# Fixed background steps late in the gate and up product, a sine chain cut in three, and pinned first splits of the down product

## The chip, the cores and the metric

The kernel runs on one core of one Trainium2 chip. The metric is the device time of one execution in microseconds, the median of several runs. "PE" is TensorE's matmul stream, "DVE" VectorE, "ACT" ScalarE, "POOL" GpSimd and "SP" SyncE. POOL and SP are used here almost only to issue transfers.

## The reference, cut to what matters

One encoder layer on 256 tokens with 2048 features, in float32: a mixer of four groups (gated linear attention, a Fourier mixer, a long convolution and a short one), cross attention to 256 memory tokens, and a gated feed-forward of width 5632.

```python
def hyena_filters(feats, w1, b1, w2, b2, w3, freq, decay):
    h = jnp.sin(freq * (feats @ w1 + b1))
    h = jnp.sin(freq * (h @ w2 + b2))
    h = h @ w3
    ...                                   # window, and the transform of both orders

def swiglu(h, w_gate_up, w_down):
    gate, up = jnp.split(h @ w_gate_up, 2, axis=-1)
    return (jax.nn.silu(gate) * up) @ w_down

    x = x + mix @ w_out[l]
    x = x + cross_attention(rms_norm(x, norm_g[l, 1]), ...)
    x = x + swiglu(rms_norm(x, norm_g[l, 2]), w_gate_up[l], w_down[l])
return rms_norm(x, final_norm_g)
```

The two places that the change touches are the two sines of the filters (early in the kernel) and the hand-over inside `swiglu`, where the product of gate and up becomes the left operand of down.

## The kernel before, in words

**Splitting.** Every float32 product is made of three float32r matmuls: each operand is cut into a high part `h` (rounded by an ACT cast) and a low part `l` (what is left, a DVE subtraction), and PE adds `h*h`, `h*l` and `l*h`. The weights arrive as 1 MB slabs (16 blocks of 128x128) in `raw` tiles through SP's queue. A slab is two items of 1024 columns, and `Stream.split` (L140 to L149) makes an item's `wh` with ACT (L146) and its `wl` with DVE (L147). Some slabs (`seven`) are also added up with each other on DVE (L176), for products that save one matmul group in eight. `Stream.look` makes items as far ahead as there are buffers: three in pool `wp`, two more in `wp2` for the slabs of gate and up and the first two of down.

**Order.** The program is written once in Python, and a list scheduler then fixes each engine's order. Each engine works in that order and waits where an operand is not there. An instruction may be moved ahead of others that were written earlier, unless `keep_place(mark)` (L323) was called: it ties each instruction written since the mark to the one written before it on the same engine. The items of `seven` slabs are tied in this way; those of the other slabs are not.

**Background work.** Work that is not on the way of the current product is a Python generator in `Background` (L231). After each matmul group the code calls `poll`, which steps a generator whose time has come, but only while `owed`, the DVE time that was promised and not yet covered by PE time, is under 0.9. `drain` steps generators to their end, whatever is owed. `dve(n, ops)` adds n/960 + 0.155 per operation to `owed`, and `pe(us)` takes PE time off.

**Gate and up** (`gate_up`, L932). Eleven steps `j` of 512 columns each. In a step, `i` runs over eight slabs of the contraction; from `j` = 1 on, three of the eight (`i` = 1, 3, 5) are `seven` slabs. A step ends with `combine` and `finish` on DVE and ACT, which leave 512 features of silu(gate) * up, turned, in the DRAM tensor `hidden` (L507, eight POOL transfers). Three generators run beside it:
- `turned` (`turn`, L1041): sixteen DVE transposes of the residual (L1048), each followed by four POOL stores to `xrows` (L1051), and then four pairs of POOL loads back into `res` (L1055). One step of the generator is one transpose, or one pair of loads.
- `early` (`fetch`, L909): it loads `hidden` back in tiles of 128 features (L917, into one of 11 `tmp` tiles) and splits each into down's left operand `f[k]` (ACT cast L310, DVE subtraction L302). It loads three tiles ahead of the one that it splits; one step of the generator is one split, and the splits are tied by `keep_place`. It makes `f[0]` to `f[15]`; the slots are `act` and `f` tiles.
- `end` (`finish` of the step before).

**Down** (class `Down`, L1063). The plan takes `k` = 0 to 31 in plain groups of four, then six `unit`s for `k` = 32 to 43. `start` (L1178) runs the first two plain groups (`k` = 0 to 7) while the pools of gate and up are still there, and drains `end`, `turned` and `early`. `begin` (L1187) fetches `f[16]` to `f[43]` in the same manner, six ahead, and `ready(k + 4)` steps that generator before each `k`.

**The sines** (`Hyena.sine`, L1315). Nine DVE operations on 64 partitions (bias, frequency, range reduction, clamp: L1320 and L306) and an ACT sine, written in one piece and tied in their places. `filters` (L1360) calls it twice, after the matmuls of L1371 and L1384, and goes on with four transforms (`dft`, L1341, matmuls L1339).

```python
    def poll(self):
        for e in list(self.q):
            if self.owed < OWED and self.now >= e[1]:
                self.step(e)
```

Of the kernel before, what the change touches and what calls it, by code (L numbers as in the profile page):

```python
# [18 lines left out]
ALU = mybir.AluOpType  # L19
# [4 lines left out]
R = 256  # L24
# [16 lines left out]
LATE = 12  # L41

AHEAD = 2

EARLY = 16

# [2 lines left out]
def sevens(j):  # L49

    return (1, 3, 5) if j else (5,)
# [19 lines left out]
DOWN = GU // 16 + 16 * DFF // 1024  # L71
# [4 lines left out]
def seven(slab):  # L76

    j, i = divmod(slab - GU // 16, 8)
    return slab in UNITS if slab >= DOWN else j >= 0 and i in sevens(j)
# [11 lines left out]
V_B1, V_B2, V_FR = 129, 130, 131  # L91
# [3 lines left out]
TWO_PI_1 = 6.28125  # L95
TWO_PI_2 = float(np.float32(2 * math.pi - 6.28125))
TWO_PI_3 = float(2 * math.pi - 6.28125 - float(np.float32(2 * math.pi - 6.28125)))
MAGIC = float(np.float32(1.5 * 2 ** 23))
PI_LO = float(np.nextafter(np.float32(math.pi), np.float32(0)))


class Stream:
# [48 lines left out]
    def make(self):  # L151

        nc, (slab, part) = self.nc, self.todo
        n = 16 * slab + 8 * part
        if n >= NBLK - HELD:
            parts = [(self.places.pop(0)) for _ in range(2)]
            r = self.raw(slab)[:, part * 1024:part * 1024 + 1024]
            for a, (wh, wl) in zip((0, 512), parts):
                nc.scalar.copy(wh, r[:, a:a + 512])
                nc.vector.tensor_tensor(out=wl, in0=r[:, a:a + 512], in1=wh.bitcast(F32), op=ALU.subtract)  # L160
            self.bg.dve(1024, 2)
            self.items.append((None, parts))
            self.todo = (slab + part, 1 - part)
            return True
        pool = self.free(slab)
        if pool is None:
            return False
        raw = self.raw(slab)
        at = 48 if any(a <= n < b for a, b in ROWS) else 8
        r = raw[:, part % 2 * 1024:part % 2 * 1024 + 1024]  # L170
        if not seven(slab):
            self.split(pool, at, r, [0, 256, 512, 1024] if n == 0 else [0, 512, 1024] if n == 8 else [0, 1024])
            self.todo = (slab + part, 1 - part)
            return True
        mark = len(nc.cur_bb.bb.instructions)
        op = lambda out, a, b, what=ALU.subtract: nc.vector.tensor_tensor(out=out, in0=a, in1=b, op=what)  # L176
        self.split(pool, at, r, [0, 512] if part == 0 else [0, 1024])
        b11, b12, b22, b21 = (raw[:, a:a + 512] for a in range(0, 2048, 512))
        if part == 0:
            blk = raw.rearrange("p (b c) -> p b c", b=4)  # L180
            op(r.rearrange("p (b c) -> p b c", b=2), blk[:, 0:3:2, :], blk[:, 1:2, :].to_broadcast([P, 2, 512]))
            self.bg.dve(1024)
        elif part == 1:
            op(b22, b22, b11, ALU.add)
            op(b21, b21, b22)
            self.bg.dve(1024, 2)
        self.keep(mark)
        self.todo = (slab + part // 3, (part + 1) % 4)
        return True
# [41 lines left out]
class Background:  # L231
# [20 lines left out]
    def step(self, e):  # L252
        w = next(e[0], self)
        if w is self:
            self.q.remove(e)
        else:
            e[1] = self.now + self.owed + (w or LAG)

    def poll(self):
        for e in list(self.q):  # L260
            if self.owed < OWED and self.now >= e[1]:
                self.step(e)

    def drain(self, g=None, others=False):
        while True:
            q = [e for e in self.q if g is None or e[0] is g]
            if not q:
                break
            for e in list(self.q) if others else q:
                self.step(e)  # L270


class Block:
# [605 lines left out]
    def mlp(self):  # L879
        tc, nc, act, st = self.tc, self.nc, self.act, self.st  # L880
        slots = lambda pool, n, a, b: [pool.tile([P, 512], F32R, name=f"{n}{i}") for i in range(a, b)]
        with tc.tile_pool(name="fp", bufs=1) as fp:
# [3 lines left out]
            with tc.tile_pool(name="wp2", bufs=2) as wp2, tc.tile_pool(name="rawx", bufs=1) as st.rawx, \  # L886
                    tc.tile_pool(name="sw", bufs=1) as sw, tc.tile_pool(name="gp", bufs=1) as gp:
                self.gap(sw, 192)
                st.pools.append([wp2, 2, DOWN + AHEAD])
                d = Down(self, f)  # L890
# [41 lines left out]
    def gate_up(self, sw, gp, f):  # L932

        nc, st = self.nc, self.st
# [25 lines left out]
        def unit(i, cs, ps, start, stop, c0, c1):  # L960

            whole = lambda k, r: [self.h3[k][:, a + r * P:a + (r + 1) * P] for a in (0, R)]
            formed = lambda n: [x[:, n * P:(n + 1) * P] for x in sums[i]]
            for (p, a, own), b in zip(((ps[0], whole(2 * i, 0), True), (cs[0][1], formed(3), False),
                                       (cs[0][0], whole(2 * i + 1, 0), False), (ps[1], formed(0), True), (ps[2], formed(2), True),
                                       (ps[3], formed(1), True), (cs[1][0], whole(2 * i + 1, 1), False)),
                                      st.take_forms("w_gate_up", (2 * i, 2 * i + 1), c0, c1), strict=True):
                self.part(p, *a, *b, own and start, own and stop)
                self.bg.poll()
# [36 lines left out]
        turned = self.bg.add(self.turn())  # L1006
        early = end = None
        for j in range(DFF // 512):
            cols = [j * 512, DFF + j * 512]
            banks = [self.gbank, self.bank]  # L1010
            cs = [[banks[j % 2]() for _ in cols] for _ in range(2)]
            if j == 1:
                early = self.bg.add(self.fetch(f, 0, EARLY, 3, 2.0))
            for i in range(8):
                if j == 0 and i == 6:
                    for g in ready:
                        self.bg.drain(g)
                if i == 1 and end:
                    self.bg.drain(end)
                if i in sevens(j):  # L1020
                    if i == sevens(j)[0]:
                        if j == 0:
                            self.bg.drain(forms)
                        ps = [banks[1 - j % 2]() for _ in range(4)]
                    unit(i, cs, ps, i == sevens(j)[0], i == sevens(j)[-1], *cols)
                    if i == sevens(j)[-1]:
                        s = [[gp.tile([P, 512], F32, name=f"{n}{r}", tag=f"{n}{r}") for n in "gh"] for r in range(2)]
                        last = combine(ps, s)
                        self.bg.add(last)
                    continue  # L1030
                for k in (2 * i, 2 * i + 1):
                    for c in range(2):
                        wh, wl = st.take("w_gate_up", k, cols[c], 4)
                        for r in range(2):
                            self.part_rows(cs[r][c], r, self.h3[k], wh, wl, k == 0, k == KT - 1)
                            self.bg.poll()
            self.bg.drain(last)
            end = self.bg.add(finish(j, cs, s))
# [24 lines left out]
class Down:  # L1063
# [114 lines left out]
    def start(self, end, turned, early):  # L1178
# [3 lines left out]
        self.open(PLANS[0], b.bank)  # L1182
        self.run(0, PLANS[0][:AHEAD], None)
        for x in (end, turned, early):
            b.bg.drain(x)

    def begin(self, sd):  # L1187
# [5 lines left out]
        n, self.rest = (1 + max(i for i, x in enumerate(plan) if x[0] == "unit") for plan in PLANS)  # L1193
        self.run(0, one[AHEAD:n], b.gbank)
        todo = [b.bg.add(self.combine(0))]
# [61 lines left out]
class Hyena:  # L1257
# [57 lines left out]
    def sine(self, p, bias):  # L1315

        b, nc = self.b, self.b.nc
        a, n = b.tmp()[0:64, :], b.tmp()[0:64, :]
        v = lambda c: b.vec[0:64, c:c + 1]
        ts = lambda out, in0, s1, op0, s2=None, op1=None: nc.vector.tensor_scalar(  # L1320
            out=out, in0=in0, scalar1=s1, scalar2=s2, op0=op0, **({} if op1 is None else {"op1": op1}))
        b.bg.dve(6 * 200, 6)
        mark = b.mark()
        ts(a, p, v(bias), ALU.add)
        ts(a, a, v(V_FR), ALU.mult)
        ts(n, a, 1.0 / (2 * math.pi), ALU.mult)
        ts(n, n, MAGIC, ALU.add)
        ts(n, n, MAGIC, ALU.subtract)
        for c in (TWO_PI_1, TWO_PI_2, TWO_PI_3):
            b.stt(a, n, -c, a, ALU.mult, ALU.add)  # L1330
        ts(a, a, PI_LO, ALU.min, -PI_LO, ALU.max)
        nc.scalar.activation(a, a, AF.Sin)
        b.keep_place(mark)
        return a
# [25 lines left out]
    def filters(self):  # L1360
        b, nc, t = self.b, self.b.nc, self.b.t
# [7 lines left out]
        p = b.bank()  # L1369
        mark = b.mark()  # L1370
        nc.tensor.matmul(p[0:64, 0:R], c33[:, R:R + 64], c33[:, 0:R], start=True, stop=True)  # L1371
        b.keep_place(mark)
        h = self.sine(p[0:64, 0:R], V_B1)
        for _ in range(4):
            yield
        b.split2(self.tabh, self.tabl, fwd)
# [5 lines left out]
        p = b.bank()  # L1382
        mark = b.mark()
        nc.tensor.matmul(p[0:64, 0:R], w2, h, start=True, stop=True)  # L1384
        b.keep_place(mark)
        h = self.sine(p[0:64, 0:R], V_B2)
        hs = self.k2.tile([P, R], F32R, name="hs", tag="hs", bufs=1)
        nc.scalar.copy(hs[0:64, :], h)
        b.tt(hs[64:P, :], h, hs[0:64, :].bitcast(F32), ALU.subtract)
# [2 lines left out]
        for o in range(2):  # L1392
# [12 lines left out]
            for r in range(2):  # L1405
                hd = []
                for d in range(2):
                    wh, wl, dc = ws[d]
                    p = b.bank()
# [428 lines left out]
```

## Time and profile before

| what | value |
|---|---|
| median of 3 runs | 1467.46 us (1466.33 to 1468.1) |
| the profiled execution's own time | 1466.78 us |
| its span, first to last instruction | 1464.7 us |
| PE busy | 1442.2 us, 98% of the span |
| DVE busy | 1192.9 us, 81% |
| ACT busy | 842.9 us, 58% |
| POOL busy | 171.5 us, 12% |
| mean granted TensorE clock | 0.997 |

The view of stages gives, for a stretch of the span, the busy time of each engine with the number of instructions in brackets, the granted clock, the share of the DMA engines and GB/s. The view of groups has busy time, mean ns of one, and the idle time before them with what ended it. The timeline has start, duration, engine, line, operation, output and inputs, and in square brackets how long the engine sat idle before and who ended that. A matmul of 512 columns is shown as 0.39 us long, but the next one starts 0.23 us after it: they are pipelined, and the end is modelled. Gate and up run from about 752 to 1210 us, down from 1209.9 to the end.

### The profile page before, as it was taken

How to read it: one execution, taken by the hardware profiler on the slowest of the kernel's cores; microseconds unless marked ns; L12 is line 12 of the kernel's file. 1: busy time of each engine (PE TensorE's matmuls, PEld its weight loads, DVE VectorE, ACT ScalarE, POOL GpSimd, SP SyncE). 2: the span in 40 equal slices, each digit the busy share in tenths (PEclk: the TensorE clock that was granted, in tenths of full speed). 3: DMA queues.
4: the chain of work that ended last, by engine and by line, in shares of the span. 5: the costliest groups of instructions: out<-in, count | busy, mean ns of one | idle time of the engine just before them, and what ended most of it. 6: DMA issues, size and time to landing. Idle time of an engine off the chain costs nothing.

```text
span 1464.7 us, 19727 instructions
## 1 busy us (share of the span) xinstructions
PE 1442.2 (98%) x7219; PEld 1217.2 (83%) x7219; DVE 1192.9 (81%) x1748; ACT 842.9 (58%) x1250; POOL 171.5 (12%) x294
## 2 busy tenths in 40 slices
PE   9999999999999999999999999999999999899997
PEld 7878888898899888888888888888888887688886
DVE  6588768778868767877788999999999996798875
ACT  6556655466656656666565555555555555555554
POOL 0220100000000001100013252111110116100000
PEclk9999999999999999999999999999999999999999
DMA  9976564454636555545566787556565667465554
GB/s 349 354 255 205 202 212 166 151 185 155 209 126 209 197 199 201 191 165 183 191 209 206 246 278 248 203 203 230 200 220 211 229 213 239 170 223 181 228 201 144
DMA packets 57393, 307.16 MB, mean 210 GB/s; under 512 B 9773, under 2 KB 11470, under 8 KB 25680
## 3 DMA queue, kind: packets, MB, share of 16 engines
q1 hardware_dynamic: 45920, 281.11, 54.7%
q0 software_dynamic: 10944, 24.14, 5.5%
q8 instruction: 56, 0.92, 0.2%
q10 hardware_dynamic: 432, 0.66, 0.1%
q14 instruction: 41, 0.34, 0.1%
HBM read 291.71 MB, written 14.16 MB: 209 GB/s over the span
## 4 chain that ended last, share of the span: by engine, by line
PE 93%; DMA 2%; DVE 2%; POOL 1%; issue 1%; ACT 1%; SPq 0%; POOLq 0%; ACTq 0%; DVEq 0%
PE pg L424 18%; PE pg L476 13%; PE pg L477 13%; PE pg L475 13%; PE pg L425 10%; PE pm L477 6%; PE pm L476 6%; PE pm L475 6%; DMA tmp<-hidden 1%; PE pm L1339 1%; DVE wl L147 1%; PE pg L421 1%; PE pg L422 1%; PE pm L872 1%; PE pm L845 1%
## 5 line engine op out<-in xcount | busy, mean ns | idle before, releaser
L146 ACT CAST wh<-raw 128x1024 fp32r<-128x1024 f32 (+1 forms) x589 | 590.4, 1013 | 469.6 <-PE pg L477 154.3
L147 DVE TENSOR_TENSOR wl<-raw,wh 128x1024 fp32r<-128x1024 f32 (+1 forms) x589 | 683.5, 1175 | 178.4 <-ACT wh L146 171.6
L424 PE MATMUL pg<-act,wh 128*128 128x512 f32 x1104 | 387.6, 393 | 0.0
L425 PE MATMUL pg<-act,wl 128*128 128x256 f32 x1216 | 340.7, 280 | 0.0
L476 PE MATMUL pg<-wl,act 128*128 128x512 f32 (+1 forms) x689 | 268.3, 389 | 3.3 <-DVE wl L147 3.2
L475 PE MATMUL pg<-wh,act 128*128 128x512 f32 (+1 forms) x689 | 268.4, 390 | 0.5 <-ACT wh L146 0.5
L477 PE MATMUL pg<-wh,act 128*128 128x512 f32 (+1 forms) x689 | 268.2, 389 | 0.0
L424 PEld LDWEIGHTS pg<-act,wh 128*128 128x128 f32 x1104 | 207.3, 188 | 44.9
L425 PEld LDWEIGHTS pg<-act,wl 128*128 128x128 f32 x1216 | 228.5, 188 | 0.8 <-DVE wl L147 0.5
L476 PEld LDWEIGHTS pg<-wl,act 128*128 128x128 f32 x689 | 129.4, 188 | 31.8 <-DVE wl L147 5.1
L475 PEld LDWEIGHTS pg<-wh,act 128*128 128x128 f32 x689 | 129.3, 188 | 28.2 <-issue 0.8
L477 PEld LDWEIGHTS pg<-wh,act 128*128 128x128 f32 x689 | 129.3, 188 | 27.3 <-issue 0.4
L477 PE MATMUL pm<-wh,act 128*128 128x512 f32 x318 | 123.9, 390 | 0.7 <-DVE act L302 0.6
L475 PE MATMUL pm<-wh,act 128*128 128x512 f32 x318 | 123.8, 389 | 0.0
L476 PE MATMUL pm<-wl,act 128*128 128x512 f32 x318 | 123.7, 389 | 0.0
L176 DVE TENSOR_TENSOR raw<-raw 128x1024 f32<-128x1024 f32 x129 | 111.7, 866 | 3.1
L507 POOL DMA_DIRECT2D hidden<-u x88 | 56.6, 651 | 279.7 <-DVE u L504 257.2
L477 PEld LDWEIGHTS pm<-wh,act 128*128 128x128 f32 x318 | 59.7, 188 | 13.8 <-DVE act L302 1.5
L475 PEld LDWEIGHTS pm<-wh,act 128*128 128x128 f32 x318 | 59.7, 188 | 12.6 <-ACT act L310 0.3
L476 PEld LDWEIGHTS pm<-wl,act 128*128 128x128 f32 x318 | 59.7, 188 | 12.4
L1051 POOL DMA_DIRECT2D xrows<-tmp x64 | 36.9, 585 | 154.4 <-DVE rc L306 126.6
L475 PE MATMUL pm<-wh,f 128*128 128x512 f32 x80 | 32.1, 401 | 3.2 <-ACT f L310 3.2
(353 smaller groups left out, 1764.4 us busy)
## 6 DMA issues: line engine op xcount, KB each, us to landing
raw<-in_W SPq DMA_DIRECT2D x246, 1024.0 KB, 5.0
raw<-in_W SPq DMA_DIRECT2D x11, 512.0 KB, 7.6
hidden<-u POOLq DMA_DIRECT2D x88, 64.0 KB, 4.2
tmp<-hidden POOLq DMA_DIRECT2D x44, 128.0 KB, 5.0
res<-in_xT SPq DMA_DIRECT2D x8, 512.0 KB, 5.6
k<-in_mem SPq DMA_DIRECT2D x8, 256.0 KB, 6.9
k<-in_x SPq DMA_DIRECT2D x8, 256.0 KB, 7.0
keys<-k POOLq DMA_DIRECT2D x32, 64.0 KB, 5.1
```

The costliest lines, as they stand in the source:

```text
L146: nc.scalar.copy(wh[:, a:b], r[:, a:b])
L147: nc.vector.tensor_tensor(out=wl[:, a:b], in0=r[:, a:b], in1=wh[:, a:b].bitcast(F32), op=ALU.subtract)
L176: op = lambda out, a, b, what=ALU.subtract: nc.vector.tensor_tensor(out=out, in0=a, in1=b, op=what)
L421: self.nc.tensor.matmul(p[:, 0:R], wh, slot[:, 0:R], start=start, stop=False)
L422: self.nc.tensor.matmul(p[:, 0:R], wh, slot[:, R:512], start=False, stop=False)
L424: self.nc.tensor.matmul(p[:, :], wh, slot[:, :], start=start, stop=False)
L425: self.nc.tensor.matmul(p[:, 0:R], wl, slot[:, 0:R], start=False, stop=stop)
L475: self.nc.tensor.matmul(p, hi, wh, start=start, stop=False)
L476: self.nc.tensor.matmul(p, hi, wl, start=False, stop=False)
L477: self.nc.tensor.matmul(p, lo, wh, start=False, stop=stop)
L507: nc.gpsimd.dma_start(to[:, :, 32 * a:32 * a + 32], u[32 * a:32 * a + 32, :].rearrange("f (b t) -> f b t", t=32))
L1051: nc.gpsimd.dma_start(to[:, :, c:c + 32], u[32 * a:32 * a + 32, :].rearrange("t (b f) -> t b f", f=32))
```

## The change

Four edits.

1. `Background.nudge(g)` steps generator `g` once, whatever is owed, if it is not finished. In gate and up, from `j` = 5 (`NUDGE`) to 10, `turned` is nudged ahead of slab `i` = 2, and `early` ahead of slabs `i` = 4 and `i` = 7: six and twelve fixed steps.
2. `Stream.make` ties the ordinary splits of down's first four slabs (`DOWN` to `DOWN + 3`) in their written places.
3. `sine` becomes a generator: three operations, three, then three, with a `yield` after each group, and the ACT sine after the last. The DVE time that it declares changes from `dve(1200, 6)` to three times `dve(750, 3)`.
4. `filters` calls it with `yield from`.

```diff
+NUDGE = 5
...
         if not seven(slab):
+            mark = len(nc.cur_bb.bb.instructions)
             self.split(pool, at, r, [0, 256, 512, 1024] if n == 0 else [0, 512, 1024] if n == 8 else [0, 1024])
+            if DOWN <= slab < DOWN + 2 * AHEAD:
+                self.keep(mark)
...
+    def nudge(self, g):
+        for e in [e for e in self.q if e[0] is g]:
+            self.step(e)
...
             for i in range(8):
+                if j >= NUDGE and i in (2, 4, 7):
+                    self.bg.nudge(turned if i == 2 else early)
...
-        b.bg.dve(6 * 200, 6)
+        turns = lambda *cs: [b.stt(a, n, -c, a, ALU.mult, ALU.add) for c in cs]
+        for step in (lambda: [ts(a, p, v(bias), ALU.add), ts(a, a, v(V_FR), ALU.mult), ts(n, a, 1.0 / (2 * math.pi), ALU.mult)],
+                     lambda: [ts(n, n, MAGIC, ALU.add), ts(n, n, MAGIC, ALU.subtract), turns(TWO_PI_1)],
+                     lambda: [turns(TWO_PI_2, TWO_PI_3), ts(a, a, PI_LO, ALU.min, -PI_LO, ALU.max)]):
+            mark = b.mark()
+            step()
+            b.bg.dve(3 * 250, 3)
+            b.keep_place(mark)
+            yield
         mark = b.mark()
-        ts(a, p, v(bias), ALU.add)
...
-        for c in (TWO_PI_1, TWO_PI_2, TWO_PI_3):
-            b.stt(a, n, -c, a, ALU.mult, ALU.add)
-        ts(a, a, PI_LO, ALU.min, -PI_LO, ALU.max)
         nc.scalar.activation(a, a, AF.Sin)
...
-        h = self.sine(p[0:64, 0:R], V_B1)
+        h = yield from self.sine(p[0:64, 0:R], V_B1)
```

More of the change, by code (lines that the diff above doesn't have):

```diff
@@ L1321, in sine @@
             out=out, in0=in0, scalar1=s1, scalar2=s2, op0=op0, **({} if op1 is None else {"op1": op1}))
-        b.bg.dve(6 * 200, 6)
-        mark = b.mark()
-        ts(a, p, v(bias), ALU.add)
[L1325 to L1328, printed above, removed]
-        for c in (TWO_PI_1, TWO_PI_2, TWO_PI_3):
-            b.stt(a, n, -c, a, ALU.mult, ALU.add)
-        ts(a, a, PI_LO, ALU.min, -PI_LO, ALU.max)
+        turns = lambda *cs: [b.stt(a, n, -c, a, ALU.mult, ALU.add) for c in cs]
[7 more added lines that the diff above has]
+            yield
+        mark = b.mark()
         nc.scalar.activation(a, a, AF.Sin)
@@ L1385, in filters @@
         b.keep_place(mark)
-        h = self.sine(p[0:64, 0:R], V_B2)
+        h = yield from self.sine(p[0:64, 0:R], V_B2)
         hs = self.k2.tile([P, R], F32R, name="hs", tag="hs", bufs=1)
```

## The prediction, made before the changed kernel was run

> **What bounds the kernel now.** I read the page first, then the view of waits for PE alone, then the view of stages.
>
> ```profile
> span 1464.7 us, 19727 instructions
> PE 1442.2 (98%) x7219; PEld 1217.2 (83%) x7219; DVE 1192.9 (81%) x1748; ACT 842.9 (58%) x1250; POOL 171.5 (12%) x294
> ```
>
> PE works 98% of the span. The change removes no matmul, so it can only win back PE's idle time, and only 22.5 us (1464.7 - 1442.2) of it exist; some stand at the start and the end, which the change does not touch. The waits say who ends the rest.
>
> ```profile
> PE pg L476 <- DVE wl L147: 4.0, 4, 1.6
> PE pm L475 <- ACT f L310: 3.2, 2, 1.8
> PE pm L477 <- DVE f L302: 2.9, 2, 2.7
> ```
>
> The columns are us in total, times, longest. PE waits for weights (`wl`) and for down's left operand (`f`). The stages show where.
>
> ```profile
> 64.00:102.00 38.00, 36.43 (x158) 28.68 (x157) 28.02 (x56) 24.99 (x42) 7.57 (x12) 1.00 0.84 290
> ...
> 800.00:1207.00 407.00, 407.00 (x1798) 337.11 (x1797) 385.29 (x432) 228.56 (x248) 80.05 (x130) 1.00 0.66 225
> 1207.00:1265.00 58.00, 51.13 (x210) 39.57 (x208) 36.48 (x68) 28.44 (x56) 27.08 (x48) 0.97 0.68 232
> 1265.00:1285.00 20.00, 17.06 (x72) 13.08 (x72) 20.00 (x32) 12.74 (x17) 0.00 (x0) 1.00 0.39 137
> 1285.00:1456.00 171.00, 171.00 (x755) 141.22 (x753) 141.32 (x173) 91.56 (x111) 0.00 (x0) 1.00 0.55 199
> ```
>
> The second figure is PE. Gate and up has no idle time in 407 us, and down has none after 1285. The hand-over, 1207 to 1285, has 6.87 + 2.94 = 9.81 us, and the stretch of the first sine 1.57. These two places are what the change can win.
>
> Next I followed the hand-over's waits on PE's timeline and from there to POOL's.
>
> ```profile
> 1228.50 0.39 PE L476 MATMUL pm<-wl,f 128*128 128x512 f32 x1
> 1228.72 0.39 PE L477 MATMUL pm<-wh,f 128*128 128x512 f32 x1
> 1230.89 0.50 PE L475 MATMUL pm<-wh,f 128*128 128x512 f32 x1 [1.78 <-ACT f L310]
> ...
> 1231.85 0.50 PE L477 MATMUL pm<-wh,f 128*128 128x512 f32 x1 [0.21 <-DVE f L302]
> ...
> 1238.60 0.50 PE L475 MATMUL pm<-wh,f 128*128 128x512 f32 x1 [1.46 <-ACT f L310]
> ...
> 1250.22 0.57 PE L477 MATMUL pm<-wh,f 128*128 128x512 f32 x1 [2.72 <-DVE f L302]
> 1250.59 0.63 PE L475 MATMUL pm<-wh,f 128*128 128x512 f32 x1
> 1251.01 0.63 PE L476 MATMUL pm<-wl,f 128*128 128x512 f32 x1
> ```
>
> ```profile
> 1205.88 0.58 POOL L917 DMA_DIRECT2D tmp<-hidden  x1 [24.81 <-ACT wh L146]
> 1215.28 2.31 POOL L1051 DMA_DIRECT2D xrows<-tmp  x4 [8.81 <-DVE tmp L1048]
> 1217.79 5.13 POOL L507 DMA_DIRECT2D hidden<-u  x8 [0.20 <-issue]
> 1222.91 2.30 POOL L1051 DMA_DIRECT2D xrows<-tmp  x4
> 1225.20 0.58 POOL L917 DMA_DIRECT2D tmp<-hidden  x1
> ...
> 1230.84 1.09 POOL L1055 DMA_DIRECT2D res<-xrows  x2 [2.02 <-DMA xrows<-tmp]
> 1231.92 3.23 POOL L917 DMA_DIRECT2D tmp<-hidden  x6
> 1237.41 0.55 POOL L917 DMA_DIRECT2D tmp<-hidden  x1 [2.27 <-DMA res<-xrows]
> ```
>
> Down uses an `f[k]` every 6 matmuls, 1.36 us at 0.227 each (1228.50 to 1228.72). POOL issues `f[14]`'s load at 1225.20, behind the last transposes' stores, and PE waits for it at 1228.72. The load of `f[18]` goes out at 1231.92, behind a pair of `res` loads that wait 2.02 us for those stores, and PE waits again. So the first waits come from work that was put off until the hand-over: the last two transposes (eight `xrows` stores after 1215) and the tail of the fetch.
>
> ```profile
> 876.00:1197.00 321.00, 0.00 (x0) 1.00 0.63 218
> ...
> L310 ACT CAST f<-tmp x10: 392/401/404, 1209.7 to 1231.4; 128x256 fp32r<-128x256 f32 x10
> L310 ACT CAST act<-tmp x6: 390/402/405, 1197.8 to 1212.5; 128x256 fp32r<-128x256 f32 x6
> ```
>
> The first row is ACT busy on L310 alone: no `f` split runs in 321 us, and then sixteen in 34. The reason is in the code. From `j` = 1 on, the planner counts 41.4 us of DVE per step (0.155 + n/960 for every operation) against 41.5 us of PE, so `owed` hardly falls under 0.9 and `poll` stays shut.
>
> **The change part by part.**
>
> *The sine (term A).* Before:
>
> ```profile
> 69.91 0.48 DVE L1320 TENSOR_SCALAR tmp<-pm,vec 64x256 f32<-64x256 f32 x1 [1.36 <-PE pm L1371]
> ...
> 73.73 0.24 DVE L1320 TENSOR_SCALAR tmp<-tmp 64x256 f32<-64x256 f32 x1
> 73.90 0.70 DVE L504 STREAM_TRANSPOSE k<-pg 128x512 f32<-128x512 f32 x1
> 74.53 2.31 DVE L147 TENSOR_TENSOR wl<-raw,wh 128x1024 fp32r<-128x1024 f32 x2
> ```
>
> The chain holds DVE from 69.91 to 73.97, with two transposes in it or behind it, and the `wl` that PE needs at 74.03 starts at 74.53 and takes about 1.15. In three pieces a third of it (about 1.3 us) stands ahead of that `wl`, which then ends near 72.5. The wait goes: 1.57 us, and about 0.16 more, since the idle column counts from the modelled end (0.39) and the next matmul would have started after 0.23. Term A: **-1.7**. The second sine is already interleaved and PE did not wait for it. Its cost: each `yield` waits for `owed` plus 1.3 us, so both sines together come some 13 us later, and the filters' last transform, whose matmuls end at 166.3, comes near 179, inside the last value product.
>
> ```profile
> 172.00:195.00 23.00, 23.00 (x103) 19.06 (x102) 16.20 (x24) 15.55 (x28) 2.13 (x4) 1.00 0.65 222
> ```
>
> DVE is idle 6.8 of 23 us there, so I take nothing, with 4 us as the upper bound (the last transforms drained in one burst).
>
> *The fixed steps (terms B and C).* By the trace two splits and fourteen transposes are done by `j` = 4. Six nudges make the last two transposes and move the `res` loads up; twelve nudges make `f[2]` to `f[13]`. So POOL loses 8 stores (4.6 us) and the waits of 2.02 and 2.27 at the hand-over, and ACT and DVE lose twelve splits. With the 11 `tmp` tiles free, `f[14]` to `f[24]` can be loaded before 1215. Without waits `f[k]` is needed at 1209.9 + 1.36k: `f[14]` at 1229, `f[18]` at 1234, `f[24]` at 1243. All of these are then there, so the waits at 1228, 1231, 1236 and 1247 go: 1.78 + 0.21 + 1.46 + 2.72 = 6.17, and 0.2 more for each of the three long ones. After the last of them the clock drops:
>
> ```profile
> 1250.50:1253.90 3.40, 3.40 (x9) 2.68 (x9) 3.40 (x11) 1.15 (x3) 2.08 (x4) 0.50 0.86 287
> ```
>
> Matmuls start 0.43 apart (1250.59 to 1251.01) instead of 0.227, eight of them: 1.6 us. Term B: **-8.4**. [...]
>
> What is late next is the fetch beyond `f[24]`, where a load must wait for a freed `tmp` tile. ACT takes its casts in a fixed order:
>
> ```profile
> 1248.77 0.41 ACT L310 CAST act<-tmp 128x256 fp32r<-128x256 f32 x1 [5.22 <-DMA tmp<-hidden]
> ```
>
> A cast for the units stands ahead of `f[24]`'s and blocks ACT while its load lands (5 to 6 us after issue), and the same happens twice more before 1264. The other waits (9.81 - 6.17 = 3.64 idle, six of them, 4.6 with the 0.16 each) follow from it: `wh` and `wl` queue behind such casts. An earlier fetch shortens this loop but the 11 tiles and the order remain. Bounds: all 4.6 gone, or none. I take half: term C **-2.5**.
>
> *What the fixed steps cost in gate and up.*
>
> ```profile
> 838.00:879.30 41.30, 41.30 (x184) 34.22 (x183) 40.31 (x50) 23.31 (x27) 20.03 (x34) 1.00 0.74 251
> 1086.70:1128.20 41.50, 41.50 (x185) 34.38 (x184) 38.99 (x44) 23.19 (x27) 5.13 (x8) 1.00 0.62 216
> ...
> L1048 DVE STREAM_TRANSPOSE tmp<-res x16: 401/434/439, 760.2 to 1218.0; 128x256 f32<-128x256 f32 x16
> L302 DVE TENSOR_TENSOR f<-tmp,f 128x256 fp32r<-128x256 f32 x20 | 7.5, 418 | 5.8 <-ACT f L310 5.8
> ```
>
> A late step has DVE busy 39.0 of 41.5. Two splits (0.42 each) and at most one transpose (0.43) make it 40.3. Step 1 of before had 40.31 with five transposes and a split in it, and PE was busy all 41.30. So the cover is 2.5 us of DVE per step, and the cost 0. POOL, busy 5.13 of 41.5, hides 4 stores and 2 loads. If the cover were gone, the price is 12 x 0.42 + 2 x 0.43 = 5.9 us.
>
> *The tie on down's first splits.* Eight items stay behind what was written before them on ACT and DVE, at worst `finish` (8 operations of 0.69, 5.5 us). Five items of 2.72 us each stand ready, so I take 0; bounds -0.5 (a split no longer overtakes an `f`) and +2.7 (one item late).
>
> *Sum.* -1.7 - 8.4 - 2.5 = -12.6. The profiled execution took 1466.78, 2.1 more than its span, so 1454.2. The median of the runs is 0.7 above it: **1455**.
>
> **The rivals.**
> 1. *The fetch is late anyway* (chance 0.17): the 11 tiles and ACT's order keep the waits from 1247 on. Only A and the first three waits go: 1.7 + 3.45 + 0.4 = 5.5, so 1462. For it: ACT's 5.22 us wait. Against: that load left at 1242, after 4.3 us of POOL waits that go.
> 2. *The filters' tail* (0.10): the drain at the end of the value product emits it in one burst, 4 us of PE wait: 1459. Against: DVE's 6.8 idle us.
> 3. *Slower: the ties in gate and up stall DVE* (0.12). A tied `f` cast stands on ACT behind the `wh` cast written before it, which can wait up to 2.72 us for PE to free a buffer; DVE, tied as well, waits for that cast. Two such waits per step plus 1.3 us of work, less the cover of 2.5, are 4.2 us per step, 25 in six steps: 1467 - 13 + 25 = 1479. It decides for slower from 1.6 us of wait per split, where the loss of six steps reaches 12.6. Against: the two splits that before has in steps 0 and 1 cost PE nothing.
> 4. *The change does not do what it says* (0.06): the scheduler moves the nudged work back, or other transfers hold `tmp`, and the hand-over stays: 1466 to 1468.
>
> **How the numbers follow.** The forecast (1451.5 to 1458.5) has 0.55. Faster takes it with rivals 1 and 2: 0.82. Same, within 0.2% (3 us, about what a measurement of this kernel can tell from no change), is rival 4: 0.06. Slower is rival 3: 0.12. The low end, 1451.5, is all 14.7 us won (1452.8) and 1.3 for the spread of the runs; the high end, 1463, takes in rivals 1 and 2. That leaves out 0.18.
>
> **What would show it.** A right: no `wl` wait near 74, and DVE's L1320 in three groups. B right: `f` casts spread over `j` = 5 to 10, no `xrows` store after 1190, PE without a wait for `f` until 1243, and no stretch at half clock before the end. C: the waits of L476 for `wl` behind ACT casts, half as long. Rival 3 would show as PE idle between 960 and 1207. A PE wait near 195 speaks for rival 2.

## The result, and the profile after

The changed kernel takes **1459.79 us** (median of five runs, 1459.27 to 1462.38) against 1467.25 for the kernel before on the same chip (five runs, 1466.33 to 1468.1). The ratio is 0.9954, with a 95% interval of 0.994 to 0.9969. The profiled execution took 1459.79 with a span of 1458.0, so it is 7.0 shorter than the one before (1466.78). The forecast of 12.6 less was 5.6 too much. The time lies 1.3 above the forecast's own band (1451.5 to 1458.5) and inside the range up to 1463, whose upper part was there for rivals 1 and 2.

The busy times on the page after, and the view of waits for PE (us in total, times, longest):

```profile
PE 1441.3 (99%) x7219; PEld 1218.0 (84%) x7219; DVE 1191.4 (82%) x1748; ACT 843.7 (58%) x1252; POOL 172.3 (12%) x294
```

```profile
PE pg L485 <- DVE wl L149: 3.9, 4, 1.5
PE pm L484 <- ACT act L319: 1.2, 1, 1.2
```

The waits for `f` (3.2 + 2.9 before) are not in the list any more. What PE waits for now are weights, `wl` for 3.9 as against 4.8 (before had, beside the 4.0, a row of 0.8 with `pm`), and `act` tiles, which at this point hold down's left operand. The stages of after (the second figure is PE, then PE's weight loads, DVE, ACT, POOL):

```profile
64.00:102.00 38.00, 36.53 (x159) 28.74 (x158) 26.34 (x53) 21.26 (x36) 8.12 (x13) 1.00 0.82 283
800.00:1207.00 407.00, 407.00 (x1797) 337.11 (x1797) 387.74 (x445) 230.76 (x259) 92.34 (x151) 1.00 0.66 230
1207.00:1265.00 58.00, 54.05 (x226) 42.67 (x225) 39.46 (x69) 30.73 (x53) 15.51 (x27) 0.97 0.56 194
```

In the stretch of the first sine PE's idle time went from 1.57 to 1.47: nothing was won there. Gate and up has PE busy 407 of 407 still, with DVE up from 385.29 to 387.74 and POOL from 80.05 to 92.34. The hand-over's idle time fell from 9.81 to 3.95 (PE is busy all 20.00 between 1265 and 1285), and POOL's busy time in it from 27.08 to 15.51. PE's timeline shows what is left of the first part of the hand-over:

```profile
1248.22 0.39 PE L486 MATMUL pm<-wh,f 128*128 128x512 f32 x1
1249.83 0.50 PE L484 MATMUL pm<-wh,act 128*128 128x512 f32 x1 [1.22 <-ACT act L319]
1250.17 0.40 PE L485 MATMUL pm<-wl,act 128*128 128x512 f32 x1
1251.12 0.51 PE L486 MATMUL pm<-wh,act 128*128 128x512 f32 x1 [0.56 <-DVE act L311]
```

I measure the losses from here on as the distance between two starts less the 0.227 that it has without a wait: 1249.83 - 1248.22 - 0.23 = 1.38, and 0.72 for the second. In this way the hand-over of before lost 13.2 (the forecast's 6.17 + 0.6 for the waits for `f`, 1.6 at half clock, 4.6 for the rest, and 0.2 in small ones); that of after loses 1.38 + 0.72, then 1.4 at half clock (seven starts of 0.43 instead of 0.227 between 1251.8 and 1254.8), then 1.52 + 0.99 for `wl` and 0.15, together 6.2. The difference is the whole 7.0.

POOL's timeline of before and after, in the second half of the hand-over (xcount loads of `hidden`, and in brackets what the queue waited for):

```profile
1253.41 1.62 POOL L917 DMA_DIRECT2D tmp<-hidden  x3 [0.70 <-DVE f L302]
1258.49 1.08 POOL L917 DMA_DIRECT2D tmp<-hidden  x2 [3.45 <-DVE act L302]
```

```profile
1220.91 1.13 POOL L926 DMA_DIRECT2D tmp<-hidden  x2
...
1243.34 1.09 POOL L926 DMA_DIRECT2D tmp<-hidden  x2 [4.55 <-DVE f L311]
...
1246.29 1.62 POOL L926 DMA_DIRECT2D tmp<-hidden  x3 [0.70 <-DVE f L311]
1251.36 1.08 POOL L926 DMA_DIRECT2D tmp<-hidden  x2 [3.45 <-DVE act L311]
```

Nineteen loads are left after 1215, so `f[0]` to `f[24]` had been loaded by then, as forecast. But compare the last two rows with those of before: the same groups with the same waits, 7.1 earlier, and 5.07 or 5.08 apart in both (1246.29 to 1251.36, 1253.41 to 1258.49). The tail of the fetch was not shortened, it was only moved. On ACT's timeline of after it looks like this:

```profile
1241.64 0.41 ACT L319 CAST act<-tmp 128x256 fp32r<-128x256 f32 x1 [2.49 <-DMA tmp<-hidden]
...
1248.12 0.41 ACT L319 CAST act<-tmp 128x256 fp32r<-128x256 f32 x1 [3.05 <-DMA tmp<-hidden]
...
1249.38 1.01 ACT L319 CAST act<-tmp 128x256 fp32r<-128x256 f32 x3
...
1256.16 0.41 ACT L319 CAST act<-tmp 128x256 fp32r<-128x256 f32 x1 [3.81 <-DMA tmp<-hidden]
1256.47 1.04 ACT L148 CAST wh<-raw 128x1024 fp32r<-128x1024 f32 x1
```

Three times a cast waits for a tile that a load brings, 9.35 in all, and weight casts and the three casts of 1249.38, the first of which PE waits for at 1249.83, queue behind it.

### The profile page after: what moved, and what is told of

Same layout as the page of the kernel before. It is cut to its first block, busy times and chain, and to the rows that moved or that the text cites. A ratio compares the mean times of both kernels' runs of the same rounds, so it can differ in the third digit from the quotient of the medians.

```text
span 1458.0 us, 19733 instructions
## 1 busy us (share of the span) xinstructions
PE 1441.3 (99%) x7219; PEld 1218.0 (84%) x7219; DVE 1191.4 (82%) x1748; ACT 843.7 (58%) x1252; POOL 172.3 (12%) x294
## 4 chain that ended last, share of the span: by engine, by line
PE 94%; issue 2%; DVE 1%; DMA 1%; POOL 1%; ACT 1%; SPq 0%; DVEq 0%; POOLq 0%; ACTq 0%
PE pg L433 18%; PE pg L485 13%; PE pg L486 13%; PE pg L484 13%; PE pg L434 10%; PE pm L485 6%; PE pm L484 6%; PE pm L486 6%; PE pm L1350 1%; DMA tmp<-hidden 1%; DVE wl L149 1%; PE pg L430 1%; PE pg L431 1%; PE pm L881 1%; PE pm L854 1%
## 5 line engine op out<-in xcount | busy, mean ns | idle before, releaser
L926 POOL DMA_DIRECT2D tmp<-hidden x44 | 24.5, 561 | 151.4 <-DVE f L311 87.4
```

The lines of the kernel that those rows point to most:

```text
L926: self.nc.gpsimd.dma_start(m[k], self.ff[k * P:(k + 1) * P, :])
```

## The experiments

Two questions were open: which edits make the 7.0, and why terms A and C brought nothing. Where C's loss comes from I had two theories. **C1**: ACT's fixed order, in which a unit's cast stands ahead of plain casts. **C2**: the loop of tiles and ties: the splits are tied in their places and run at PE's pace, a split frees a `tmp` tile, and only then does the next load go out.

### Which edit makes the gain

The sine in three pieces alone, on the kernel before (edits 3 and 4).

> The kernel before with the sine chain in three pieces and nothing else. Theory A (the prediction): the nine DVE operations hold back the weight split at 74, so in three pieces PE's wait of 1.5 us near 74 goes, ratio 0.9988. Theory B (from the changed kernel's trace): the two key transposes stand ahead of that split in DVE's order and wait for PE until 73.2, so the wait near 74 stays at 1.4 to 1.6 us and the time at 1467, ratio 0.9995 to 1.0005.

Measured: 1466.22, ratio 1.0001 [0.9992, 1.0009]. DVE's timeline of this run shows why:

```profile
71.30 0.29 DVE L1320 TENSOR_SCALAR tmp<-tmp 64x256 f32<-64x256 f32 x1
73.60 1.40 DVE L504 STREAM_TRANSPOSE k<-pg 128x512 f32<-128x512 f32 x2 [2.01 <-PE pg L477]
74.92 2.32 DVE L147 TENSOR_TENSOR wl<-raw,wh 128x1024 fp32r<-128x1024 f32 x2
```

After the first piece DVE stands idle for 2.01. Next in its order come two transposes of keys that wait for the end of a PE group at 73.6, and only then the `wl`. Before, the sine's other six operations filled that idle time. So cutting the sine alone cannot win: behind its first piece the transposes hold `wl` to the same moment. No run ties the transposes with the sine left in one piece, so what the sine would cost without them is not shown.

The eighteen fixed steps alone (edit 1), and the ties on down's first splits alone (edit 2).

> The kernel before with the eighteen fixed steps alone (no ties, sine in one piece). If the whole gain is theirs: 1460, 7 us under before, no PE wait for f until 1245, PE waits of some 5 us left between 1245 and 1265. If the ties of down's first splits carry part of it, the waits near 1228 to 1237 come back in part and the time is 1462 or more.

> The kernel before with down's first splits tied in their places and nothing else. My theory: nothing, 1467, the same waits at 1228, 1237 and 1247. Rival: the ties put the splits behind f's casts or ahead of them, and the hand-over changes by 1 us or more either way.

Measured: the steps 1459.41, ratio 0.995 [0.9938, 0.9963]; the ties 1467.57, ratio 1.0007 [0.9998, 1.0016]. The steps are the whole change. The ties move waits about: the view of waits has one of 4.1 for a weight cast and one of 1.9 for an `f`, where before had four of 1.78, 0.21, 1.46 and 2.72:

```profile
PE pm L478 <- ACT wh L146: 4.1, 1, 4.1
PE pm L480 <- DVE f L305: 1.9, 1, 1.9
```

The profiled execution is the slowest of this run's eleven (1469.78). Its waits change place, but their sum hardly does (6.0 against 6.17), so the run says only that the ties win nothing.

The two kinds of steps, each alone on the kernel before.

```diff
+                if j >= NUDGE and i == 2:
+                    self.bg.nudge(turned)
```

> The kernel before, with the six fixed steps of the residual's turn alone. POOL loses eight xrows stores (4.6) and the two waits for them at the hand-over, but the twelve splits stay there. If POOL's queue set the first waits, those at 1228 to 1238 go and the later ones stay: 1462 to 1464. If the splits' order on ACT and DVE set them, less than 1 goes: 1466.

```diff
+                if j >= NUDGE and i in (4, 7):
+                    self.bg.nudge(early)
```

> The kernel before, with the twelve fixed steps of the fetch alone. The f tiles up to f[24] are loaded before the last transposes' stores, so the waits before 1243 go, but the loads from the 25th on stand behind eight stores and the res loads, and the waits after 1243 grow: 1461 to 1464. If the two kinds of steps are worth the same and add up, this and the run before it win 3 to 5 each.

Measured: the turn's steps alone 1459.38, ratio 0.9954 [0.9941, 0.9968]; the fetch's alone 1460.6, ratio 0.9962 [0.995, 0.9975]. Both beat what I expected, and they do not add: either gives about all of it. The run with the turn's six steps tells what mattered. ACT's and DVE's splits stay at the hand-over there (groups between 1195 and 1225), and still no wait for `f` is left; POOL has no `xrows` store after 900, and its loads at the hand-over come without one between them:

```profile
L316 ACT CAST f<-tmp 128x256 fp32r<-128x256 f32 x8 | 2.7, 397 | 0.0
L316 ACT CAST act<-tmp 128x256 fp32r<-128x256 f32 x6 | 2.1, 403 | 0.0
```

```profile
1214.14 2.69 POOL L923 DMA_DIRECT2D tmp<-hidden  x5 [1.98 <-DVE act L308]
1218.02 5.16 POOL L513 DMA_DIRECT2D hidden<-u  x8 [1.19 <-DVE u L510]
1223.18 2.75 POOL L923 DMA_DIRECT2D tmp<-hidden  x5
```

So the first waits came from what the turn had in POOL's queue ahead of the fetch (eight stores, the first of them behind 8.81 of waiting for its transpose, and `res` loads that wait for the stores), and not from the splits that were put off. In the run with the fetch's steps alone the turn moved as well, without being stepped: its last store left by 1086.1 instead of 1224.6. Here is the one line of its summary.

```profile
L1059 POOL DMA_DIRECT2D xrows<-tmp x24: 582/582/611, 1040.6 to 1086.1; - x24
```

That run therefore does not separate the two causes.

### Why term A brought nothing

The changed kernel with the key transposes tied in their written places, so that they cannot be put ahead of `wl`.

```diff
     def store_turned(self, to, u, src, tied=False):
+        mark = self.mark()
         nc.vector.transpose(u, src)
+        if tied:
+            self.keep_place(mark)
```

All three key groups first:

> The changed kernel, with the transposes of the keys tied behind the weight splits that were written before them. Theory B: the split that PE needs at 74 then runs during DVE's 2 us of waiting, PE's wait near 74 goes, and the time is 1.6 us under the changed kernel (1458). Theory A has no room for it: with the chain in three pieces nothing else should hold the split, and the time stays at 1460. The risk for B: the transposes come up to 8 us later, and a later product waits for their PSUM banks.

Measured: 1460.96, ratio 0.9962 [0.9949, 0.9974], a miss. The wait near 74 is gone, but the first group's transposes now free their `pg` tiles late, and PE waits for that at 53:

```profile
PE pg L484 <- DVE k L514: 2.0, 1, 2.0
```

Then the second group alone (`tied` where `c == 1024`):

> The changed kernel, with the transposes of the second key group alone (the two that stand ahead of wl near 74) held in their written places. If the wait near 74 is only DVE's order there, and the new wait at 53 of the run before came from tying the first group, the wait near 74 goes, nothing new comes, and the time is 1.6 under the changed kernel: 1458.2. If the transposes are late wherever they stand (the PSUM bank they free is needed soon), a new wait of 1 to 2 appears at 75 to 85 and the time stays at 1459.8.

Measured: 1458.17, ratio 0.9943 [0.993, 0.9955], 1.6 under the changed kernel's 1459.79, with no wait between 70 and 100. DVE's timeline:

```profile
70.79 0.29 DVE L1334 TENSOR_SCALAR tmp<-tmp 64x256 f32<-64x256 f32 x1
71.00 2.35 DVE L149 TENSOR_TENSOR wl<-raw,wh 128x1024 fp32r<-128x1024 f32 x2
```

Now `wl` starts at 71.0, right behind the sine's first piece, as the forecast had it. The intervals of this run and of the changed kernel overlap, so the 1.6 rests on the trace as well: the 1.63 that PE of the changed kernel loses between 73.67 and 75.75 is not there.

### Why term C brought nothing

C1's edit: the splits for the units are tied behind the plain splits that were written before them.

```diff
+                        mark = self.mark()
                         form(i - 1, m.pop(i - 1), m.pop(i))
+                        self.keep_place(mark)
```

> The changed kernel, with the splits for the units (form) tied behind the plain splits that were written before them. Theory C1 (ACT's fixed order: a unit's cast stands ahead of the plain f and weight casts and blocks ACT while its load lands): the waits of act at 1248 and 1250 and the half clock behind them go, 1.4 + 0.7 + 1.4 = 3.5 less, 1456.3, perhaps also a part of the 2.5 at 1260. Theory C2 (the loop of 11 tmp tiles: a load may go out only when a split frees a tile, and the splits are tied at PE's pace): the same losses stay within 1 us, in other places, 1459 to 1460.

Measured: 1464.08, ratio 0.9983 [0.9974, 0.9991], 4.3 above the changed kernel. The waits for `act` and the half clock near 1250 went, as C1 has it, and PE is busy 57.93 of the 58 up to 1265. But the weights of the units came late instead, and the loss moved behind 1265:

```profile
1207.00:1265.00 58.00, 57.93 (x256) 47.50 (x255) 42.85 (x65) 28.88 (x46) 15.51 (x27) 1.00 0.64 217
1265.00:1285.00 20.00, 15.38 (x57) 10.96 (x56) 16.17 (x25) 9.85 (x13) 0.00 (x0) 0.91 0.43 157
```

```profile
PE pg L484 <- ACT wh L148: 5.6, 5, 2.5
```

C1 is right about who stands ahead of whom at 1248, but this reorder wins nothing. What holds the units' weights back in it I have not shown.

C2's edit: the splits of `f[16]` and on (the fetch of `begin`) are not tied any more.

```diff
-                self.keep_place(mark)
+                if k1 == EARLY:
+                    self.keep_place(mark)
```

> The changed kernel, with the splits of f[16] and on no longer tied to the instruction written before them. C2: the splits come as soon as their tiles have landed, free their tmp tiles some 8 us earlier, the loads from the 27th on go out earlier and the waits for act go: 1455 to 1457. C1 alone: the casts stand in ACT's order ahead of weight casts and wait there for the two buffer sets, a new wait of up to 4 for wh at 1220 to 1235: 1460 to 1464.

Measured: **1454.88**, ratio 0.9918 [0.9905, 0.9932], 4.9 under the changed kernel. ACT's and POOL's timelines:

```profile
1216.84 2.86 ACT L319 CAST f<-tmp 128x256 fp32r<-128x256 f32 x9 [3.19 <-issue]
```

```profile
1221.99 4.36 POOL L926 DMA_DIRECT2D tmp<-hidden  x8
...
1239.68 0.55 POOL L926 DMA_DIRECT2D tmp<-hidden  x1 [2.00 <-ACT act L319]
```

Nine casts run in a stretch in which ACT of the changed kernel sat idle for 5.92 (up to 1218.50, ahead of a weight cast that waited for PE). They free nine tiles, and eight loads go out at 1222 instead of two. The last load leaves at 1239.68 instead of 1254.51. Of the 6.2 lost in the hand-over about 1.3 are left.

The number of tiles: the changed kernel with 9 `tmp` tiles (`pool("tp", 9)`).

> The changed kernel with 9 instead of 11 tmp tiles. C2: two loads fewer can be under way, each load from the 25th on goes out one pair (2.72 us) later, and the losses of the hand-over grow by 3 to 6: 1463 to 1466, with the first wait before 1245. C1: the order of ACT decides, not the tiles: within 1 us of 1459.8.

Measured: 1456.79, ratio 0.9933 [0.9919, 0.9947]. Two tiles fewer made it 3.0 *faster*, which neither theory has. In its POOL timeline the pairs of loads go on every 2.72, where those of the changed kernel stop between 1237.70 and 1243.34:

```profile
1240.80 1.09 POOL L926 DMA_DIRECT2D tmp<-hidden  x2 [1.64 <-DVE f L311]
```

The list scheduler wrote another order with fewer tiles: there is no unit cast ahead of the plain ones near 1241, and the first one waits 5.05 at 1247.30. Its last load even leaves later (1256.79 against 1254.51). So the run moves the tiles and the order together and does not isolate the tiles: it shows that two tiles fewer need cost nothing, and that a later last load does not by itself make a later end. For C2 this leaves the half that speaks of the ties, which rests on the run before. More than 11 tiles, or 9 in the order of the changed kernel, were not tried.

Last, C2's edit on the kernel before, with none of the change.

> The kernel before, with the splits of f[16] and on not tied, and none of the change. Theory C2 (the ties pace the fetch, but the put-off work, eight xrows stores and sixteen casts after 1207, stands ahead of it): the waits for f[14] and f[18] at 1228 to 1238 stay and only the later ones shrink: 1461 to 1464. If the ties alone were the cause of the whole hand-over, it comes near 1456 and the fixed steps were not needed.

Measured: 1463.62, ratio 0.9981 [0.9972, 0.999]. The waits for `f` at the stores stay (1.8 and 1.0), and only the later one goes:

```profile
PE pm L475 <- ACT f L310: 2.8, 2, 1.8
```

Untying wins 2.3 here, and 4.9 once the steps have emptied POOL's queue. The two are in series: a queue first, and behind it an order.

### Both edits that won

> The changed kernel with both edits that won: the transposes of the second key group tied, and the splits of f[16] and on not tied. The two touch stretches 1100 us apart, so their gains (1.6 and 4.9) should add: 1453.2, with no wait near 74 and less than 2 left between 1207 and 1285. If the untied splits win only by a lucky order, another start of the same program brings waits back: 1455 to 1458.

Measured: **1451.15** (1450.38 to 1452.53), ratio 0.99 [0.9887, 0.9914]: 14.8 under the kernel before and faster than both kernels. The gain over the changed kernel is 8.6 (7.9 by the two ratios to the kernel before), where 6.5 was the sum of the two; part of the rest is the last wait for `wl` in the hand-over, where PE lost 0.92 with the splits untied alone (from 1258.41) and 0.43 here (from 1254.47). PE is busy 57.72 of the 58 up to 1265 and all 20.00 up to 1285, so the untied splits win again in another program, and their gain does not hang on one lucky order. Of PE's waits for weights in the view of this run this is all that is left (3.9 in the changed kernel):

```profile
PE pg L485 <- DVE wl L149: 0.5, 2, 0.3
```

## Why the prediction was right or wrong

| step | forecast | measured |
|---|---|---|
| A, the wait for `wl` near 74 | -1.7 | -0.1 |
| B, the four waits for `f` | -6.8 | -6.8 |
| B, the stretch at half clock | -1.6 | -0.2 |
| C, half of the rest of the hand-over | -2.5 | +0.2 |
| gate and up; ties on down | 0; 0 | 0; 0 |
| sum | -12.6 | -6.9 (-7.0 by the execution's own time) |

**B's waits: right in place and size, and only half right in the reason.** All four went, and no `xrows` store or `f` wait was left. The forecast gave the cause to both kinds of put-off work. The run with the turn's steps alone shows that taking the turn's transfers out of POOL's queue was enough, and the twelve steps of the fetch were not needed. In that queue the forecast counted the stores' 4.6 and the waits of 2.02 and 2.27, and overlooked the 8.81 that POOL sat ahead of the first store, at 1215.28; in the run with the turn's steps eight loads go out between 1206 and 1217.

**A failed in the step "in three pieces a third of it stands ahead of that `wl`".** I read the two transposes inside the chain as passengers of it. The row for them gives no releaser because the sine was still running when their PE group ended; take the sine away, and the same row shows 2.02 of waiting for PE. The first line of what would show it (no `wl` wait near 74) came out against A, and its second line (L1320 in pieces) came out for it: the edit does what it says, and nothing was limited by the sine alone.

**B's half clock failed as a price.** I took the slow stretch as 1.6 on top of the waits. Compare the changed kernel with the run of the fetch's steps alone, whose waits at 1248 and 1250 are nearly the same (1.22 and 0.56, 1.19 and 0.56). One has the clock at half and no wait until 1260; the other has the full clock and then loses 0.29 at 1253.7 and 1.03 at 1257.4. Behind it both lose 1.5 and 1.0 for `wl` and go on within 0.2 us of the same moment. Here are these two waits in the changed kernel, and in the run with the fetch's steps alone:

```profile
1261.84 0.50 PE L485 MATMUL pg<-wl,act 128*128 128x512 f32 x1 [1.35 <-DVE wl L149]
...
1264.32 0.49 PE L485 MATMUL pg<-wl,s 128*128 128x512 f32 x1 [0.82 <-DVE wl L149]
```

```profile
1261.66 0.50 PE L482 MATMUL pg<-wl,act 128*128 128x512 f32 x1 [1.37 <-DVE wl L149]
...
1264.15 0.50 PE L482 MATMUL pg<-wl,s 128*128 128x512 f32 x1 [0.81 <-DVE wl L149]
```

From the start behind the first wait to the last of these starts it is 14.49 at half clock and 14.35 at full clock. Two more runs have waits of 1.2 and 0.56 there: the turn's steps alone take 14.53 at full clock, the eighteen steps alone 14.89 at half clock. So at most some 0.5 of the 1.4 comes through. In this stretch, which ends when weights arrive, the slow PE mostly filled time in which it would have waited. The forecast should have put the clock at nothing, or nearly so, there.

**C failed in the step "an earlier fetch shortens this loop".** The tail is a chain of its own (tied split, freed tile, load, unit cast, weight cast), and it moved 7.1 earlier as it stood. The order that I named is there, as the run with the tied units shows. What set the pace were the ties of the later splits: without them the time falls by 4.9. That this is about my upper bound for C (4.6) is chance, since the bound was for another edit. Whether more tiles would have loosened the chain as well stays open.

**The rivals.** Rival 1 (the fetch is late anyway) came nearest, with its 1462 and with its mechanism: waits from 1248 on stayed, though the wait of 2.72 went, and A did not come. The range held the time because it took in this rival. Of the gains that the forecast counted only B's waits came. Rival 2 did not happen (no PE wait near 195: PE is busy 23.00 of the 23 between 172 and 195). Rival 3 did not either: the cover of DVE in gate and up was enough. The edit that does nothing (rival 4) describes edits 2 to 4, but not the steps.

## What to carry to other kernels

Before pricing a wait, ask what the engine that ends it would do next if the work ahead of it were gone: an instruction that shows no wait may be standing behind one. Where a stretch ends with the arrival of its supply, neither PE's waits nor a slow clock in it can be added up (here at most some 0.5 of the 1.4 at half clock came through): find the chain that supplies it and shorten that. Ties that keep an order also keep its pace, so try them one by one, and look for engines that sit idle just ahead of tied work.

## What the runs showed of the hardware

The granted clock halved after one pair of waits, and stayed at 1.00 after a pair of nearly the same lengths. Here are the same two stretches of PE in the changed kernel, and in the run with the fetch's steps alone (the figure after the bracket is the granted clock):

```profile
1247.50:1251.50 4.00, 2.22 (x9) 1.00 0.41 137
1251.50:1255.00 3.50, 3.50 (x10) 0.51 0.87 314
```

```profile
1247.50:1251.50 4.00, 2.25 (x9) 1.00 0.42 133
1251.50:1255.00 3.50, 3.36 (x15) 1.00 0.91 315
```

In both PE idles 1.2 and then 0.56 us (2.22 and 2.25 busy of 4.00), and only the first is then slow for about 3 us (0.51 against 1.00 in the second row). In the kernel before, more idle time than in either, 1.78 and 0.21 us (PE busy 1.40 of the 3.40 from 1228.50), left the clock at 1.00 in the 3.40 behind it. In these three places neither the longest wait nor the sum of the idle time tells whether the clock drops, and no run shows what does.
